# Sums of output-weight blocks by accumulating DRAM transfers; one sweep over both column halves

## The chip, the cores and the metric

The kernel runs on one core of a Trainium2 chip. The metric is the device time of one execution in microseconds; the median of several runs is given. An execution is also recorded by the profiler, and the views below are of such a recorded execution. The engines are called as the profile does: PE is TensorE (PEld its weight loads), DVE is VectorE, ACT is ScalarE, POOL is GpSimd, SP is SyncE, which here only issues transfers.

## The reference

One layer of a decoder trunk over 512 tokens of width 2048. The normalised input, modulated by a conditioning vector, goes through one input projection. Half of its columns feed a state-space (SSD) branch, half a retention branch. Both results side by side are 4096 wide, go through one output projection, are gated, added to the residual and normalised again.

```python
u = rms_norm(h, norm_w) * (1.0 + scale) + shift
proj = u @ w_in
z, xbc, dt_raw, q, k, v, g = jnp.split(proj, ...)
y_ssd = gated_group_rms_norm(ssd_chunked(...) + xs * d_skip, z, ssd_norm_w)
y_ret = head_group_norm(retention_chunked(...), ret_norm_w) * jax.nn.silu(g)
mixed = jnp.concatenate([y_ssd, y_ret], axis=-1) @ w_out     # (512, 4096) @ (4096, 2048)
h = h + gate[:, None, :] * mixed
return rms_norm(h, final_norm_w)
```

## The kernel before

All matrix products run in fp32 split in two: each operand is a high part (`hi`, the value cast to the matmul's fp32 form, on ACT) and a low part (`lo`, the rest, a subtraction on DVE). `mm3` multiplies hi by hi, hi by lo and lo by hi, three matmuls of 128 x 128 by 128 x 512 each.

The program text gives what is computed and in which buffers. A scheduler then orders each engine's instructions ahead of time on a simulated timeline: the earlier one in the text goes first, but one that is ready and has a buffer may go ahead of others that still wait. On the chip each engine runs its own list strictly in order, and waits where an operand is not there.

**Input projection** (`unit`, L109). A unit is 512 output columns. For each of 8 pairs of 128 rows of weight, `load_w` (L91) lets SP load 512 KB into one of three `raw` buffers, ACT writes one of four `hi`, DVE one of four `lo`; 24 matmuls follow. Nineteen units run through `unit`: first those of the SSD groups 1 to 3, each followed by `ssd_a` and `ssd_b`, then for each of four pairs of retention heads `qk`, `v` and `g` with `ret_a`, `ret_b` and `ret_c`. During the `v` units `gate_part` (L537) also loads the gate's weights through the `raw` buffers. POOL does short work for these branches: the decay loads `dec` from DRAM (L372), roots (L75, L76), the second half of the rotary sums (L439).

**Forms.** The output projection multiplies by a scheme with seven block products instead of eight (Strassen in Winograd's form). The operand of 4096 columns is taken in 16 blocks j of 256 columns, each with two halves of columns and two halves of tokens: A11, A12, A21, A22. `put_mix` (L327) builds the sums of these on POOL and stores them to DRAM (`mixd`): AS holds A11 and A21 - A22; SR, S2, A12 and A22 the others.

**Output projection** (L728 to L810). The 2048 output columns are taken as two halves q of 1024, and for each the whole scheme is run: per half 16 blocks, in each seven products of two row tiles. Three stretches follow each other for one q:

- a first loop with banks Y, Z and W: two neighbouring weight blocks are loaded into one `raw` of 512 KB, POOL adds them in place (L743) and makes the next sum `t2` from it (L748), then they are split (`split`, L698) and multiplied; `t2` stays in SBUF;
- a second loop: POOL adds a block to `t2` (L764) and builds another sum in `raw` (L770); the products add to Y, Z and W;
- a third loop multiplies A22 by `t2` into banks X.

The forms are loaded and split by `m_pair` (L711) in every stretch, once for each q: 112 splits of 128 x 512. `finish` (L659) multiplies by the gate, adds the residual and takes the sum of squares; `weighted` (L673) and `store` (L676) apply the last norm and send the row to DRAM. The finished tiles `h` have 16 buffers in the pool `res`, which opens when the branches' buffers are released.

Of the kernel before, what the change touches and what calls it, by code (L numbers as in the profile page):

```python
# [18 lines left out]
P = 128  # L19
# [22 lines left out]
def hybrid_block(ctx, tc, x, c_row, vecs, heads, w_mod, w_gate, b_gate, w_in, w_dt, w_out, fnw,  # L42
# [47 lines left out]

    def load_w(src, width, eng=dve):  # L91
        raw = wp.tile([P, 2, width], F32, tag="raw", bufs=3, name="raw")
        sp.dma_start(raw.rearrange("p k f -> p (k f)"), src)
        hi = wp.tile([P, 2, width], F32R, tag="hi", bufs=4, name="hi")
        lo = wp.tile([P, 2, width], F32R, tag="lo", bufs=4, name="lo")
        act.copy(hi, raw)  # L96
        eng.tensor_tensor(lo, raw, hi.bitcast(F32), ALU.subtract)  # L97
        return hi, lo
# [10 lines left out]
    def unit(name, w_stationary, tag="mm", side=None):  # L109
# [190 lines left out]
    def conv_silu(pb, ct, tag, bufs, name, r=None):  # L300
# [5 lines left out]
        for j in range(1, 4):  # L306
# [10 lines left out]
            for f, n in (("AS", 2 * QJ), ("SR", 2 * QJ), ("S2", QJ), ("A12", QJ), ("A22", QJ))}  # L317
# [9 lines left out]
    def put_mix(i, src, nw):  # L327
# [13 lines left out]
        s2 = t2k("xd", 2, "ms", (P, 256))  # L341
        pool.tensor_tensor(g[:, 0, :], a11, a21, ALU.subtract)
        pool.tensor_tensor(a21, a21, a22, ALU.subtract)
        pool.tensor_tensor(s2, a21, a11, ALU.subtract)
        pool.tensor_tensor(g[:, 1, :], a12, s2, ALU.add)
        pool.dma_start(mixd["AS"][j].rearrange("p a t -> p (a t)"), ma)
        pool.dma_start(mixd["SR"][j], g)
        pool.dma_start(mixd["S2"][j // 2][:, j % 2, :], s2)
        pool.dma_start(mixd["A12"][j // 2][:, j % 2, :], a12)
        pool.dma_start(mixd["A22"][j // 2][:, j % 2, :], a22)  # L350

# [300 lines left out]
    for n in range(4):  # L652
        fw = res.tile([P, 512], F32, tag=f"fw{n}", name=f"fw{n}")
        pool.dma_start(fw, fnw[n * 512:(n + 1) * 512].partition_broadcast(P))
        fws.append(fw)
# [3 lines left out]
    def finish(t, n, c, more=None):  # L659

        xr = t2k("zs", 4, "xr")
        sp.dma_start(xr, x[t * P:(t + 1) * P, n * 512:(n + 1) * 512])
        h = res.tile([P, 512], F32, tag="h", bufs=16, name=f"h{t}_{n}")
        if more is not None:
            dve.tensor_tensor(h, c, more, ALU.add)
            c = h
        dve.tensor_tensor(h, c, gate[n], ALU.mult)
        dve.tensor_tensor(h, h, xr, ALU.add)
# [4 lines left out]
    def weighted(t, n):  # L673
        dve.tensor_tensor(hout[t][n], hout[t][n], fws[n], ALU.mult)

    def store(t, late):  # L676
# [4 lines left out]
        for m in [late] + [m for m in range(4) if m != late]:  # L681
            h = hout[t][m]
            if m == late:
                dve.scalar_tensor_tensor(h, h, rs, fws[m], ALU.mult, ALU.mult)
            elif m == late ^ 1:
                dve.tensor_scalar(h, h, rs, None, ALU.mult)
            else:
                act.activation(h, h, AF.Copy, scale=rs)
# [9 lines left out]
    def split(dst, src, eng=dve):  # L698
        act.copy(dst[0], src)  # L699
        eng.tensor_tensor(dst[1], src, dst[0].bitcast(F32), ALU.subtract)  # L700

    def w_raw(q, jj, at):
        raw = wp.tile([P, 2, 512], F32, tag="raw", bufs=3, name="raw")
        sp.dma_start(raw.rearrange("p k f -> p (k f)"),
                     w_out[QJ * q + jj][:, at * 512:(at + 2) * 512])
        return raw

    def w_pair():
        return [wp.tile([P, 2, 512], F32R, tag=tg, bufs=4, name=tg) for tg in ("hi", "lo")]

    def m_pair(src):  # L711
        mr = t2k("xs", 5, "mr")
        sp.dma_start(mr, src.rearrange("p a t -> p (a t)"))
        mh = up.tile([P, 512], F32R, tag="ul", bufs=NK + 1, name="mh")
        ml = up.tile([P, 512], F32R, tag="ul", bufs=NK + 1, name="ml")
        split((mh, ml), mr)
        return mh, ml

    def mul(banks, m, i, w, k, first, last, rows=(0, 1), more=False):

        for t in rows:
            sl = slice(i * 256 + t * P, i * 256 + (t + 1) * P)
            mm3(banks[t], (m[0][:, sl], m[1][:, sl]), (w[0][:, k, :], w[1][:, k, :]), first, last, more)

    def kept_tile(tag):
        return res.tile([P, 512], F32, tag=tag, bufs=2, name=tag)

    for q in range(2):  # L728
        n0, n1 = 2 * q, 2 * q + 1
        by = [bank("mm", f"Y{t}") for t in range(2)]  # L730
        bz = [bank("mm", f"Z{t}") for t in range(2)]
        bw = [bank("aux", f"W{t}") for t in range(2)]
        t2s = []
        for jj in range(QJ):
            ms2 = m_pair(mixd["S2"][jj])
            t2w = w_pair()
            for e in range(2):
                first, last = jj == e == 0, jj == QJ - 1 and e == 1
                t2 = up.tile([P, 512], F32, tag="uh", bufs=NK, name="t2")
                sp.dma_start(t2, w_out[QJ * q + jj][:, (5 if e else 2) * 512:(6 if e else 3) * 512])  # L740
                raw = w_raw(q, jj, 6 * e)
                m = m_pair(mixd["AS"][2 * jj + e])
                pool.tensor_tensor(raw[:, 1 - e, :], raw[:, 0, :], raw[:, 1, :], ALU.add)  # L743
                w = w_pair()
                split(w, raw)
                mul(by, m, 0, w, e, first, last)
                mul(bw, m, 1, w, 1 - e, first, last)
                pool.tensor_tensor(t2, t2, raw[:, 1 - e, :], ALU.add)  # L748
                split([v[:, e, :] for v in t2w], t2)
                mul(bz, ms2, e, t2w, e, first, last)  # L750
                t2s.append(t2)
        e1, u2, w1 = ([kept_tile(tg) for _ in range(2)] for tg in ("e1", "u2", "w1"))
        for t in range(2):
            act.copy(e1[t], by[t])
            dve.tensor_tensor(u2[t], bz[t], e1[t], ALU.add)
            act.copy(w1[t], bw[t])
        for jj in range(QJ):
            raw = w_raw(q, jj, 3)
            m = m_pair(mixd["A12"][jj])
            w = w_pair()  # L760
            split(w, raw)
            for e in range(2):
                t2 = t2s[2 * jj + e]
                pool.tensor_tensor(t2, t2, raw[:, e, :], ALU.add)  # L764
                mul(by, m, e, w, e, False, jj == QJ - 1 and e == 1, more=True)
            for e in range(2):
                last = jj == QJ - 1 and e == 1
                raw = w_raw(q, jj, 5 if e else 1)
                m = m_pair(mixd["SR"][2 * jj + e])
                pool.tensor_tensor(raw[:, e, :], raw[:, 0, :], raw[:, 1, :], ALU.add)  # L770
                w = w_pair()
                split(w, raw)
                mul(bz, m, 0, w, e, False, last, more=True)
                mul(bw, m, 1, w, 1 - e, False, last, more=True)
        for t in range(2):
            finish(t, n0, by[t])
        for t in range(2):
            dve.tensor_tensor(e1[t], bz[t], e1[t], ALU.add)
            dve.tensor_tensor(u2[t], bw[t], u2[t], ALU.subtract)
            pool.tensor_tensor(w1[t], w1[t], e1[t], ALU.subtract)  # L780
            finish(t, n1, u2[t])
            finish(2 + t, n1, w1[t])
        if q:
            for t in range(2):
                weighted(t, n0)
                store(t, n1)
        bx = [bank("aux", f"X{t}") for t in range(2)]
        held = []
        for jj in range(QJ):
            m = m_pair(mixd["A22"][jj])  # L790
            w = w_pair()
            for e in range(2):
                split([v[:, e, :] for v in w], t2s[2 * jj + e])
            held.append((jj, m, w))
            if q and QJ - 3 <= jj < QJ - 1:
                continue
            for t in range(2):
                for jj_, m, w in held:
                    for e in range(2):
                        mul(bx, m, e, w, e, jj_ == e == 0, jj_ == QJ - 1 and e == 1, (t,))  # L800
            held = []
        for t in range(2):
            finish(2 + t, n0, bx[t], e1[t])
            if q:
                weighted(2 + t, n1)
                store(2 + t, n0)
        if not q:
            for t in range(NC):
                weighted(t, n0)
                weighted(t, n1)  # L810
# [27 lines left out]
def _quads(w):  # L838


    k, n = w.shape
    b = w.reshape(k // 512, 2, 2, P, n // 1024, 2, 512).transpose(4, 0, 3, 1, 2, 5, 6)
    order = [(0, 0, 0), (0, 0, 1), (0, 1, 1), (0, 1, 0), (1, 1, 0), (1, 1, 1), (1, 0, 1), (1, 0, 0)]
    return np.stack([b[:, :, :, e, i, j] for e, i, j in order], axis=3).reshape(-1, P, 8 * 512)
# [49 lines left out]
```

## Time and profile before

| | us |
|---|---|
| median of 3 runs | 1538.67 (1538.36 to 1545.83) |
| the profiled execution | 1534.36 |
| its span | 1532.6 |
| PE busy | 1448.2 |
| DVE busy | 1035.2 |
| ACT busy | 570.6 |
| POOL busy | 546.8 |
| bytes moved by all transfers | 263.30 MB |

A row of the groups reads: line, engine and operation, what is written and read with its shape, how often, then busy time in us and the mean ns of one, then the idle time of the engine just before these instructions and what ended it. A row of the waits reads: who waited, for what, us in total, how often, the longest. In the timeline the first two numbers are start and duration. A busy PE is not PE at its peak: a matmul of 512 columns is shown as 0.39 us long, but the next starts 0.23 us later.

### The profile page before, as it was taken

To read this page: it belongs to the slowest core of one execution; us is meant where nothing else is said; L and a number is where in the kernel's file an instruction comes from. 1 tells how busy PE (TensorE), PEld (TensorE's weight loads), DVE (VectorE), ACT (ScalarE), POOL (GpSimd) and SP (SyncE) were. 2 spreads that over 40 slices of the span, in tenths; PEclk is the share of its full clock that TensorE was granted. 3 is DMA by queue.
4 is the path that set the end of the run, shared out by engine and by line. 5 is a ranking of instruction groups with operands and counts; after the bars stand their busy time and mean duration, and the time that the engine had idled before them with its cause. 6 is when DMAs were issued, how large, how long until landed. Compare 5 with 4: busy or idle time off the path is not lost.

```text
span 1532.6 us, 17621 instructions
## 1 busy us (share of the span) xinstructions
PE 1448.2 (94%) x6481; PEld 1169.3 (76%) x6481; DVE 1035.2 (68%) x1160; ACT 570.6 (37%) x816; POOL 546.8 (36%) x512
## 2 busy tenths in 40 slices
PE   6988999999999999999999999999998898878895
PEld 4766887778888888888888888888886666656774
DVE  6899777775564574543544364336458998999897
ACT  6423443534433432223121322132235445544454
POOL 4540015562054144101300220022037767266662
PEclk9999999999999999999999999999999999999998
DMA  9888442534234225523552444245466677756763
GB/s 359 327 306 287 148 124 81 166 116 145 90 116 145 96 79 176 179 74 106 167 169 83 145 156 139 83 145 169 150 206 228 229 241 248 240 181 196 247 193 138
DMA packets 82810, 263.30 MB, mean 172 GB/s; under 512 B 10145, under 2 KB 10321, under 8 KB 78625
## 3 DMA queue, kind: packets, MB, share of 16 engines
q1 hardware_dynamic: 73298, 233.98, 46.7%
q0 software_dynamic: 8272, 26.08, 4.9%
q10 hardware_dynamic: 1152, 2.10, 0.4%
q8 instruction: 51, 0.84, 0.2%
q14 instruction: 37, 0.30, 0.1%
HBM read 243.18 MB, written 18.94 MB: 171 GB/s over the span
## 4 chain that ended last, share of the span: by engine, by line
PE 60%; DVE 12%; DMA 4%; POOL 4%; issue 3%; ACT 2%; POOLq 0%; DVEq 0%; ACTq 0%; SPq 0%
PE acc L105 16%; PE acc L107 16%; PE acc L106 16%; DVE lo L700 6%; DMA raw<-w_out_d 4%; DVE ml L700 2%; POOL raw L770 1%; PE py L390 1%; PE po L487 1%; ACT hi L699 1%; PE pT L332 1%; PE Y L106 1%; PE po L489 1%; PE pkv L508 1%; POOL t L764 1%
## 5 line engine op out<-in xcount | busy, mean ns | idle before, releaser
L97 DVE TENSOR_TENSOR lo<-raw,hi 128x1024 fp32r<-128x1024 f32 (+1 forms) x166 | 211.4, 1276 | 256.0 <-ACT hi L96 253.3
L96 ACT CAST hi<-raw 128x1024 fp32r<-128x1024 f32 (+1 forms) x184 | 186.4, 1017 | 440.9 <-PE acc L107 193.8
L106 PE MATMUL acc<-lo,uh 128*128 128x512 f32 x704 | 278.3, 395 | 0.0
L107 PE MATMUL acc<-hi,ul 128*128 128x512 f32 x704 | 276.5, 393 | 0.0
L105 PE MATMUL acc<-hi,uh 128*128 128x512 f32 x704 | 274.1, 392 | 0.4 <-ACT cr L303 0.4
L107 PE MATMUL acc<-uh,lo 128*128 128x512 f32 x512 | 200.2, 391 | 0.0
L106 PE MATMUL acc<-ul,hi 128*128 128x512 f32 x512 | 200.0, 391 | 0.0
L105 PE MATMUL acc<-uh,hi 128*128 128x512 f32 x512 | 199.9, 392 | 0.0
L700 DVE TENSOR_TENSOR lo<-raw,hi 128x1024 fp32r<-128x1024 f32 x80 | 146.1, 1827 | 14.5 <-ACT hi L699 14.3
L105 PEld LDWEIGHTS acc<-hi,uh 128*128 128x128 f32 x704 | 132.2, 188 | 27.6 <-ACT cr L303 0.6
L107 PEld LDWEIGHTS acc<-hi,ul 128*128 128x128 f32 x704 | 132.3, 188 | 27.6 <-issue 0.5
L106 PEld LDWEIGHTS acc<-lo,uh 128*128 128x128 f32 x704 | 132.2, 188 | 27.4 <-issue 0.5
L700 DVE TENSOR_TENSOR ml<-mr,mh 128x512 fp32r<-128x512 f32 x112 | 122.7, 1097 | 17.8 <-PE acc L107 11.2
L699 ACT CAST hi<-raw 128x1024 fp32r<-128x1024 f32 x80 | 84.0, 1050 | 104.3 <-POOL raw L770 68.4
L107 PEld LDWEIGHTS acc<-uh,lo 128*128 128x128 f32 x512 | 96.2, 188 | 19.6
L106 PEld LDWEIGHTS acc<-ul,hi 128*128 128x128 f32 x512 | 96.2, 188 | 19.5
L105 PEld LDWEIGHTS acc<-uh,hi 128*128 128x128 f32 x512 | 96.2, 188 | 19.4
L187 DVE SCALAR_TENSOR_TENSOR ada<-ada,csb 128x2048 f32<-128x2048 f32 x32 | 90.9, 2843 | 0.3 <-DMA ada<-w_mod_d 0.3
L550 DVE SCALAR_TENSOR_TENSOR gacc<-graw,cs,gacc 128x512 f32<-128x512 f32 x60 | 50.4, 841 | 57.2 <-DMA graw<-w_gate_d 56.1
L743 POOL TENSOR_TENSOR raw<-raw 128x512 f32<-128x512 f32 x32 | 54.7, 1710 | 82.1 <-DMA raw<-w_out_d 47.8
L75 POOL TENSOR_SCALAR mv<-mv 128x2 f32<-128x2 f32 x16 | 3.1, 191 | 204.6 <-DVE mv L496 204.6
L699 ACT CAST mh<-mr 128x512 fp32r<-128x512 f32 x112 | 68.4, 616 | 17.5 <-PE W L107 13.2
(264 smaller groups left out, 2655.4 us busy)
## 6 DMA issues: line engine op xcount, KB each, us to landing
raw<-w_out_d SPq DMA_DIRECT2D x80, 512.0 KB, 4.3
ada<-w_mod_d SPq DMA_DIRECT2D x32, 1024.0 KB, 5.8
raw<-w_in_z SPq DMA_DIRECT2D x32, 512.0 KB, 3.6
raw<-w_in_qk SPq DMA_DIRECT2D x32, 512.0 KB, 3.5
raw<-w_in_v SPq DMA_DIRECT2D x32, 512.0 KB, 3.9
graw<-w_gate_d SPq DMA_DIRECT2D x32, 512.0 KB, 3.7
raw<-w_in_g SPq DMA_DIRECT2D x32, 512.0 KB, 4.0
raw<-w_in_xs SPq DMA_DIRECT2D x24, 512.0 KB, 3.7
```

The costliest lines, as they stand in the source:

```text
L96: act.copy(hi, raw)
L97: eng.tensor_tensor(lo, raw, hi.bitcast(F32), ALU.subtract)
L105: pe.matmul(dst, lhsT=ah, rhs=bh, start=first, stop=False, skip_group_check=more)
L106: pe.matmul(dst, lhsT=ah, rhs=bl, start=False, stop=False, skip_group_check=more)
L107: pe.matmul(dst, lhsT=al, rhs=bh, start=False, stop=last, skip_group_check=more)
L187: dve.scalar_tensor_tensor(ada, ada, 0.5, csb, ALU.mult, ALU.mult, accum_out=dst)
L332: pe.transpose(pT[:, c * P:(c + 1) * P], src[c], ident)
L390: pe.matmul(py[:, hd], lhsT=dec[:, h, :], rhs=xd[:, hd], start=True, stop=True)
L550: dve.scalar_tensor_tensor(gacc, raw[:, kk, :], cs[:, k:k + 1], gacc, ALU.mult, ALU.add)
L699: act.copy(dst[0], src)
L700: eng.tensor_tensor(dst[1], src, dst[0].bitcast(F32), ALU.subtract)
L743: pool.tensor_tensor(raw[:, 1 - e, :], raw[:, 0, :], raw[:, 1, :], ALU.add)
```

## The change

The scheme and its number of matmuls stay. What changes is where the weight sums are made and how often things are split.

- **Weights in DRAM.** `_quads` lays out each block j as four tensors of 128 x 1024, B11, B12, B22 and B21, each with both column halves q side by side. `tsum` holds four sums for each j in DRAM: T1 = B11 + B12, T3 = B12 + B22, T2 = T1 + B22, T4 = T2 + B21.
- **Block sums by transfer.** `block_sums(n)` issues a staggered pipeline of six stages: SP copies B11 to T1 and B12 to T3; POOL adds B12 to T1 and B22 to T3 by an accumulating transfer; POOL copies T1 to T2; adds B22; copies T2 to T4; adds B21. `unit` calls it at every sixth weight load, and SP's copies are put behind that load in SP's list. A block enters at each call; 16 blocks are through after 21 calls.
- **Sweeps.** One pass over all 16 blocks serves both column halves and both row tiles, so there are four banks U and four banks W. The sweeps take (AS; B11, T1), (SR; T2, B22), (SA; T3, B21) for (U, W), and a last one A22 with T4 into U alone. U is not started anew: it keeps adding over all four sweeps, and what is needed of it between them is copied (`e1`, `u2`) or subtracted (`w1`).
- **Splits.** A weight is loaded and split once, 1024 wide, with no sum on POOL; a form is loaded and split once: 48 in the three sweeps and 8 in the last.
- **Buffers.** From the 25th weight on, the rings of `raw`, `hi` and `lo` have two more buffers each from `res`. `h` takes the buffers that `t2` had. `fnw` is loaded by SP during the first sweep instead of by POOL before it.
- **put_mix** writes SR and SA in place of SR, S2 and A12: the same number of additions and stores.

```diff
     def load_w(src, width, eng=dve):
...
-        sp.dma_start(raw.rearrange("p k f -> p (k f)"), src)
+        last_load[0] = sp.dma_start(raw.rearrange("p k f -> p (k f)"), src)
...
             if side is not None:
                 side(kc)
+            n = next(steps)
+            if n % 6 == 0:
+                with tc.issue_after(last_load[0].ins):
+                    block_sums(n // 6)
...
+    tsum = [[dram.tile([P, 1024], F32, name=f"T{i + 1}_{j}") for i in range(4)]
+            for j in range(2 * QJ)]
+    B11, B12, B22, B21 = (lambda j, i=i: w_out[4 * j + i] for i in range(4))
+    T1, T2, T3, T4 = (lambda j, i=i: tsum[j][i] for i in range(4))
...
+    def block_sums(n):
+        def add(dst, src):
+            pool.dma_start(dst, src, accum_op=ALU.add, max_dma_last_dim=4096)
+        stages = (
+            lambda j: (sp.dma_start(T1(j), B11(j)), sp.dma_start(T3(j), B12(j))),
+            lambda j: (add(T1(j), B12(j)), add(T3(j), B22(j))),
+            lambda j: pool.dma_start(T2(j), T1(j)),
+            lambda j: add(T2(j), B22(j)),
+            lambda j: pool.dma_start(T4(j), T2(j)),
+            lambda j: add(T4(j), B21(j)))
+        for i, stage in enumerate(stages):
+            if 0 <= n - i < 2 * QJ:
+                stage(n - i)
...
-    def finish(t, n, c, more=None):
+    def finish(t, n, c, more=None, op=ALU.add):
...
+        if n % 2:
+            dve.tensor_tensor(h, h, fws[n], ALU.mult)
...
+    ring = {"raw": (3, 2), "hi": (4, 2), "lo": (4, 2)}
+    def ring_tile(tag, dtype):
+        n, m = ring[tag]
+        used[tag] += 1
+        at = used[tag] % (n + m)
+        if used[tag] > 24 and at >= n:
+            return res.tile([P, 2, 512], dtype, tag=tag + "2", bufs=m, name=tag)
+        return wp.tile([P, 2, 512], dtype, tag=tag, bufs=n, name=tag)
...
+    def weight(src):
+        raw = ring_tile("raw", F32)
+        last_load[0] = sp.dma_start(raw.rearrange("p k f -> p (k f)"), src)
+        pair = [ring_tile(tg, F32R) for tg in ("hi", "lo")]
+        split(pair, raw)
+        return pair
...
+    for sweep, (f, wu, ww) in enumerate((("AS", B11, T1), ("SR", T2, B22), ("SA", T3, B21))):
+        if sweep != 1:
+            bw = {}
+        late = []
+        for j in range(NJ):
+            m = mixed(mixd[f][j])
+            mul(bu, m, 0, weight(wu(j)), sweep == j == 0, j == NJ - 1, sweep > 0)
...
+            late.append((j, m))
+            if sweep == 0 and j < 3:
+                continue
+            if not bw:
+                bw = {at: bank("aux", "W") for at in PAIRS}
+            for j_, m_ in late:
+                mul(bw, m_, 1, weight(ww(j_)), sweep != 1 and j_ == 0, j_ == NJ - 1, sweep == 1)
+            late = []
+        for at in PAIRS:
+            q, t = at
+            if sweep == 0:
...
+                act.copy(e1[at], bu[at])
+            elif sweep == 1:
+                u2 = res.tile([P, 512], F32, tag="u2", bufs=2, name="u2")
+                act.copy(u2, bu[at])
+                finish(t, 2 * q + 1, bw[at], u2, ALU.subtract)
+            else:
+                dve.tensor_tensor(w1[at], w1[at], bu[at], ALU.subtract)
...
+            elif sweep == 2:
+                finish(t, 2 * q, bw[at], e1[at])
+        if sweep == 2:
+            for at in PAIRS:
+                q, t = at
+                finish(2 + t, 2 * q + 1, w1[at])
+            for t in range(2):
+                store(t)
+    held = []
+    for j in range(NJ):
+        if j % 2 == 0:
+            m = mixed(mixd["A22"][j // 2])
+        held.append((j, m, weight(T4(j))))
+        if NJ - 3 <= j < NJ - 1:
+            continue
+        for at in PAIRS:
+            for j_, m_, w in held:
+                mul(bu, m_, j_ % 2, w, False, j_ == NJ - 1, True, [at])
         held = []
+    for t in range(2):
+        for q in range(2):
+            finish(2 + t, 2 * q, bu[q, t])
+        store(2 + t)
```

More of the change, by code (lines that the diff above doesn't have):

```diff
@@ L651, in hybrid_block @@
     fws = []
[L652 to L655, printed above, removed]
     sso = const.tile([P, NC, 4], F32, name="sso")
     hout = [[None] * 4 for _ in range(NC)]
-    def finish(t, n, c, more=None):
+    def finish(t, n, c, more=None, op=ALU.add):
         xr = t2k("zs", 4, "xr")
         sp.dma_start(xr, x[t * P:(t + 1) * P, n * 512:(n + 1) * 512])
-        h = res.tile([P, 512], F32, tag="h", bufs=16, name=f"h{t}_{n}")
+        h = up.tile([P, 512], F32, tag="uh", bufs=NK, name=f"h{t}_{n}")
         if more is not None:
-            dve.tensor_tensor(h, c, more, ALU.add)
+            dve.tensor_tensor(h, c, more, op)
             c = h
@@ L670, in finish, with store @@
         act.activation(jk, h, AF.Square, accum_out=sso[:, t, n:n + 1])
+        if n % 2:
+            dve.tensor_tensor(h, h, fws[n], ALU.mult)
         hout[t][n] = h
-    def weighted(t, n):
-        dve.tensor_tensor(hout[t][n], hout[t][n], fws[n], ALU.mult)
-    def store(t, late):
+    def store(t):
         rs = small.tile([P, 1], F32, name="rs")
@@ L680, in store @@
         rsqrt_into(rs, rs, 1.0 / D, EPS)
-        for m in [late] + [m for m in range(4) if m != late]:
+        for m in range(4):
             h = hout[t][m]
-            if m == late:
+            if m % 2 == 0:
                 dve.scalar_tensor_tensor(h, h, rs, fws[m], ALU.mult, ALU.mult)
-            elif m == late ^ 1:
-                dve.tensor_scalar(h, h, rs, None, ALU.mult)
             else:
@@ L711, in m_pair, with split @@
-    def m_pair(src):
+    PAIRS = [(q, t) for t in range(2) for q in range(2)]
+    ring = {"raw": (3, 2), "hi": (4, 2), "lo": (4, 2)}
+    used = dict.fromkeys(ring, 0)
+    def ring_tile(tag, dtype):
[5 more added lines that the diff above has]
+        return wp.tile([P, 2, 512], dtype, tag=tag, bufs=n, name=tag)
+    def split(dst, src):
+        act.copy(dst[0], src)
+        dve.tensor_tensor(dst[1], src, dst[0].bitcast(F32), ALU.subtract)
@@ L716, in m_pair @@
[L716 to L721, printed above, removed]
-            sl = slice(i * 256 + t * P, i * 256 + (t + 1) * P)
[L723 to L783, printed above, removed]
-            for t in range(2):
-                weighted(t, n0)
-                store(t, n1)
-        bx = [bank("aux", f"X{t}") for t in range(2)]
-        held = []
[L789 to L810, printed above, removed]
@@ new lines, in mixed, with mul @@
+        pair = [up.tile([P, 512], F32R, tag="ul", bufs=NK + 1, name=nm) for nm in ("mh", "ml")]
+        split(pair, mr)
+        return pair
+    def mul(banks, m, i, w, first, last, more=False, pairs=PAIRS):
+        for q, t in pairs:
+            sl = slice(i * 256 + t * P, i * 256 + (t + 1) * P)
+            mm3(banks[q, t], (m[0][:, sl], m[1][:, sl]), (w[0][:, q, :], w[1][:, q, :]),
+                first, last, more)
+    NJ = 2 * QJ
+    bu = {at: bank("mm", "U") for at in PAIRS}
+    bw = None
@@ L838, in _quads @@
 def _quads(w):
[L841 to L844, printed above, removed]
+    b = w.reshape(16, 2, P, 2, 2, 512).transpose(1, 4, 0, 2, 3, 5)
+    return np.stack([b[0, 0], b[0, 1], b[1, 1], b[1, 0]], axis=1).reshape(16 * 4, P, 1024)
 IN_UNITS = {"BC0": ((COL_B, 256), (COL_C, 256)), "xs0a": ((COL_XS, 256),), "z0": ((COL_Z, 512),),
@@ L875 @@
         "w_dt_d": a["w_in"][0][:, COL_DT:COL_Q].reshape(NK, P, HEADS).transpose(1, 0, 2),
-        "w_out_d": _quads(a["w_out"][0]),
         "fnw_d": a["final_norm_w"],
@@ L879 @@
     }
+    arrays["w_out_d"] = _quads(a["w_out"][0])
     for name, cols in IN_UNITS.items():
```

40 lines of the change are left out of this document (22 added, 18 removed).

## The prediction

> **What bounds the kernel now.** I read the stretches of the span first, then the waits of TensorE's weight loads, then the costliest groups, then what follows the last matmul. The columns of the first fence are: stretch, its length, then busy time and instructions of PE, PEld, DVE, ACT and POOL, the granted clock, the DMA share and GB/s.
>
> ```profile
> span 1532.6 us, 17621 instructions
> 600.00:700.00 100.00, 100.00 (x453) 83.03 (x453) 50.64 (x72) 20.85 (x23) 12.44 (x16) 1.00 0.40 127
> 1146.00:1303.00 157.00, 140.95 (x593) 108.51 (x592) 144.86 (x107) 79.32 (x114) 112.94 (x79) 0.99 0.73 237
> 1340.00:1486.00 146.00, 127.44 (x524) 99.03 (x523) 135.39 (x105) 69.35 (x99) 99.66 (x57) 0.96 0.69 215
> PEld Y L106 <- DVE lo L700: 28.9, 25, 3.0
> PEld Z L106 <- DVE lo L700: 12.7, 19, 1.4
> PEld X L106 <- DVE lo L700: 8.8, 8, 3.3
> PEld Y L105 <- ACT e L754: 6.3, 1, 6.3
> PEld Y L105 <- ACT hi L699: 4.9, 2, 4.6
> ```
>
> There are two regimes. In the input projection TensorE is busy for all of a 100 us stretch, with DVE half idle and the DMA share at 0.40: nothing can be won there, only lost. In the output projection (from 1146 us) DVE is busy 92 to 93% and TensorE is not; its weight loads wait for the `lo` half of a split. The five waits sum to 61.6 us (28.9 + 12.7 + 8.8 + 6.3 + 4.9), 50.4 of them on DVE.
>
> ```profile
> 1146.69 0.48 PE L105 MATMUL Y<-hi,mh 128*128 128x512 f32 x1
> 1157.73 0.39 PE L105 MATMUL W<-hi,mh 128*128 128x512 f32 x1
> 1161.58 0.39 PE L107 MATMUL W<-hi,ml 128*128 128x512 f32 x1
> 1516.41 0.39 PE L107 MATMUL X<-hi,ml 128*128 128x512 f32 x1
> ```
>
> Seventeen steps from 1157.73 to 1161.58 give 0.2265 us per matmul. The output projection has 2 x 16 x 14 x 3 = 1344 of them (seven block products of two row tiles, three matmuls each, 16 blocks, two column halves), so 304.4 us undisturbed. It runs from 1146.69 to 1516.8, 370.1 us. The difference, 65.7, is the waits of 61.6 and some transposes of the last heads. After the last matmul come 15.8 us of closing arithmetic and stores, which the change keeps in kind. So **the gain has a ceiling of about 62 us**.
>
> **What makes DVE late.**
>
> ```profile
> L97 DVE TENSOR_TENSOR lo<-raw,hi 128x1024 fp32r<-128x1024 f32 (+1 forms) x166 | 211.4, 1276 | 256.0 <-ACT hi L96 253.3
> L700 DVE TENSOR_TENSOR lo<-raw,hi 128x1024 fp32r<-128x1024 f32 x80 | 146.1, 1827 | 14.5 <-ACT hi L699 14.3
> L700 DVE TENSOR_TENSOR ml<-mr,mh 128x512 fp32r<-128x512 f32 x112 | 122.7, 1097 | 17.8 <-PE acc L107 11.2 <-issue 3.1 <-ACT m L334 1.9
> L700 DVE TENSOR_TENSOR lo<-t,hi 128x512 fp32r<-128x512 f32 x64 | 62.4, 1005 | 4.0 <-ACT hi L699 4.0
> L743 POOL TENSOR_TENSOR raw<-raw 128x512 f32<-128x512 f32 x32 | 54.7, 1710 | 82.1 <-DMA raw<-w_out_d 47.8 <-DMA xr<-x_d 15.6 <-DMA t<-w_out_d 12.0
> L748 POOL TENSOR_TENSOR t<-t,raw 128x512 f32<-128x512 f32 x32 | 53.5, 1675 | 2.0 <-DMA t<-w_out_d 0.3
> L764 POOL TENSOR_TENSOR t<-t,raw 128x512 f32<-128x512 f32 x32 | 56.4, 1782 | 30.5 <-DMA raw<-w_out_d 30.5
> L770 POOL TENSOR_TENSOR raw<-raw 128x512 f32<-128x512 f32 x32 | 56.1, 1760 | 17.0 <-DMA raw<-w_out_d 11.0 <-DVE lo L700 5.7
> 1488.93 1.21 DVE L700 TENSOR_TENSOR lo<-raw,hi 128x1024 fp32r<-128x1024 f32 x1
> 1490.07 0.68 DVE L700 TENSOR_TENSOR ml<-mr,mh 128x512 fp32r<-128x512 f32 x1
> ```
>
> The same subtraction takes 1276 ns in the input projection and 1827 among POOL's sums; late in the span, with POOL quiet, it is 1.21 us, and the half-wide one 0.68 instead of 1.10.
>
> **Part 1, removed.** POOL's 128 sums go (54.7 + 53.5 + 56.4 + 56.1 = 220.7 us), and with them the step "load, sum, split" becomes "load, split". Both column halves now use one split of each form: 56 form splits instead of 112. Weight splits stay equal in width: 7 x 16 = 112 of 1024, against 80 of 1024 plus 64 of 512. DVE's splits therefore go from 146.1 + 122.7 + 62.4 = 331.2 us to 112 x 1.21 + 56 x 0.68 = 174 us. The finishing operations are about 46 us, worked out below. DVE then has 220 us of work beside 304 of matmul, 72%. DVE stops being the bound and TensorE becomes it. I take 61.6 us as removed.
>
> **Part 2, added inside the output projection.** (a) Supply. Each block of a sweep needs two 512 KB weights and a 256 KB form per 24 matmuls (5.4 us), or 241 GB/s.
>
> ```profile
> raw<-w_out_d SPq DMA_DIRECT2D x80, 512.0 KB, 4.3
> q1 hardware_dynamic: 73298, 233.98, 46.7%
> L699 ACT CAST hi<-raw 128x1024 fp32r<-128x1024 f32 x80 | 84.0, 1050 | 104.3 <-POOL raw L770 68.4 <-POOL raw L743 12.7 <-DMA raw<-w_out_d 6.7
> ```
>
> A raw buffer is held 4.3 (landing) + 1.05 (cast) + 1.21 (subtraction) + about 0.7 of queueing, some 7.3 us. With three buffers that is one weight per 2.4 us, against 2.72 wanted; the first 24 weights have only these three, later ones five. It is just enough. Ends: 0 and 25 us (half of today's 50.4 on DVE); I take 6, near zero because DVE has 28% to spare.
>
> (b) The seams between sweeps. Their durations:
>
> ```profile
> L668 DVE TENSOR_TENSOR h<-h,xr 128x512 f32<-128x512 f32 x16 | 12.3, 778 | 0.0
> L674 DVE TENSOR_TENSOR h<-h,fw 128x512 f32<-128x512 f32 x12 | 8.8, 738 | 0.0
> L667 DVE TENSOR_TENSOR h<-h,gate 128x512 f32<-128x512 f32 x4 | 3.7, 955 | 0.0
> L665 DVE TENSOR_TENSOR h<-X,e 128x512 f32<-128x512 f32 x4 | 2.6, 680 | 0.0
> ```
>
> After the second sweep a finish is 0.68 + 0.955 + 0.78 + 0.74 = 3.15 us of DVE, and the fourth W bank is released after three of them and one subtraction, 10.1 us. TensorE has 12 U matmuls and three banks of W meanwhile (2.7 + 2.0). So 5.4 us are late if the order of the text is kept, 0 if the scheduler lets a further U block go first; I take 4. After the third sweep DVE has four subtractions (2.7), four finishes of 2.4, four of 2.2 and two rows to store (3.3), 24.4 us in all, ahead of the splits of the last sweep. The rings hold up to five split weights, 13.6 us of matmul, so 0 to 11 us are late. Today's two such crossings cost 8.8 us on X (row above); I take half, 4.4. After the first sweep the copies (0.6 each on ACT) fit under 12 matmuls: nothing. All finishes and stores together: 12.6 + 9.6 + 8.8 + 5.8 + 2.7 + 6.6 = 46 us.
>
> Output projection: 61.6 - 6 - 4 - 4.4 = **47 us gained**.
>
> **Part 3, added to the input projection.** Per block j: SP issues two copies, POOL six transfers (four adding, two copying), each 512 KB from DRAM to DRAM; times 16, that is 32 on SP and 96 on POOL. SP's cost nothing as far as the loads are early:
>
> ```profile
> SPq L93 <- DVE lo L97: 677.8, 133, 34.6
> 427.52 0.59 POOL L372 DMA_DIRECT2D dec<-acs_d  x1 [4.39 <-PE py L390]
> 443.29 1.90 PE L390 MATMUL py<-xd,dec 128*128 128x64 f32 x16
> dec<-acs_d POOLq DMA_DIRECT2D x16, 512.0 KB, 4.7
> POOL mv L75 <- DVE mv L496: 204.6, 16, 43.3
> ```
>
> SP waits 677.8 us for a free raw buffer. Three raw and four split pairs stand between a load and its use, so a load may be some 15 us late before TensorE sees it. That cover is thinner in the `v` units, where gate loads share the ring. Bytes: 128 transfers are 67 MB. At full share queue q1 moves 233.98 MB / (0.467 x 1532.6 us) = 327 GB/s, so copies alone would be 205 us of all engines, and 308 if an adding one counts twice. Over the 800 us in which they run that is 0.26 to 0.39 on top of about 0.38: 0.64 to 0.77, a level that the output projection runs at today (0.73).
>
> POOL pays 96 x 0.59 = 57 us of issue, in time that it waits today (204.6 us in one row alone). What stands behind these instructions on POOL are the root chains, the rotary sums and the decay loads. Now POOL also waits: each of a block's transfers needs the one before landed, so an instruction issued early holds POOL until then. A `dec` load shares the queue. It goes out at 427.52 and its matmuls run at 443.29. The chain behind it is 4.7 + 1.1 + 1.2 + 1.1 + 1.2 = 9.3 us, so about 6 us are spare: one transfer ahead is hidden, two are not. Sixteen such loads, perhaps a quarter meeting two transfers, at 2 to 5 us: some 6. For root and rotary chains behind a waiting POOL I add another 4. No row shows a DRAM to DRAM transfer or an adding one. The nearest are 4.3 and 4.7 us to land, so an adding one lies between one and two of these. Bounds of the whole part: 0 and 60 us (half of the 96 waits, each with 1.2 us of TensorE behind it); I take **10**, near the low end because a full raw ring hides most.
>
> The Trainium skill ("DMA: Bandwidth & Descriptors", Rules for kernel authors) says that an accumulating transfer reads its destination and writes it later. By it the upper byte count, 308 us, would be the right one and the sum above would not change by more than its range; no run here shows it yet.
>
> **Sum.** -47 + 10 = -37. The span goes from 1532.6 to about 1496 and the profiled execution from 1534.4 to 1497. The median of the runs shown, 1538.67, lies 4.3 above that execution, so I give 1501 for a median.
>
> **Rivals.** (1) *Adding transfers are slow.* Outside the loads' 0.38 there are 496 us of all engines in the 800; the 64 copies take 64 x 1.6 = 103 of them. Each of the 64 adding ones may then take 6.1 us, 3.8 times a copy. From there on every microsecond more costs 64, through POOL held in its waits and loads late behind them; at 7.5 us each, 90 - 47 = 43 us slower, about 1580. The same sign comes from 0.5 us of TensorE per POOL transfer (47 / 96). For it: no row shows such a transfer, and the scan chains run with little to spare. Against it: 0.6 of the DMA time is free. Chance 0.18.
>
> (2) *POOL cannot issue beside DVE.* If each issue were held for a DVE subtraction of 1.2 us, 96 x 1.2 = 115 us of POOL, perhaps a third in front of a scan: 38 us, and the gain falls to 9, about 1530. The `dec` issue of 0.59 beside a busy DVE speaks against it. The Trainium skill ("SBUF — State Buffer", the box on DVE blocking DMA) has such a rule, for descriptors of POOL's transfers while DVE holds the shared port; the row does not bear it out. Chance 0.05.
>
> (3) *The loads become the bound.* Weights and forms are 112 x 0.524 + 56 x 0.262 = 73.4 MB; at the 213 to 215 GB/s of today's second stretch they take 343 us, not 304. The gain is then 61.6 - 39 - 8 = 15, less 10: about 1534. For it: three raw buffers at first. Against: 237 GB/s at share 0.73. Chance 0.10.
>
> (4) *All hidden*: nothing lost in the input projection, few stalls, about 1480. Chance 0.12.
>
> **Chances.** Forecast (1485 to 1525) 0.55, the rivals as given. The measurement tells 0.5%, 7.7 us, from no change: faster (below 1531) is 0.55 + 0.12 and about half of (2) and (3), 0.74; within it 0.08; slower 0.18. The range runs from 1474 (the 62 us, all kept) to 1566, into rival 1.
>
> **What would show it.** After: POOL's sums gone, the `lo` subtraction near 1.21 us and `ml` near 0.68, DVE below 80% in the output projection, weight loads waiting under 20 us in all, first to last output matmul about 323 us. In the input projection TensorE still fully busy, `dec` landing under 10 us, the last input matmul at 1155 instead of 1146. A later start of the output projection by over 50 us, POOL waiting on its own transfers and a DMA share near 1 would prove me wrong, as would raw loads as the releaser of casts all through the sweeps.

## The result, and the profile after

The changed kernel is slower: 1548.54 us (median of 20 runs, 1541.25 to 1557.04) against 1536.62 (median of 20 runs of before), a ratio of 1.0075, 95% interval 1.0058 to 1.0092. The profiled span went from 1532.6 to 1545.9 us. 37 us faster was forecast.

First the page of the kernel after: span, busy time by engine, the chain that ended last (by engine, then by line), and the queues (q0 is POOL's).

```profile
span 1545.9 us, 17183 instructions
PE 1450.1 (94%) x6481; PEld 1177.1 (76%) x6481; DVE 890.8 (58%) x1064; ACT 539.5 (35%) x732; POOL 395.0 (26%) x472
PE 52%; DMA 22%; DVE 13%; issue 6%; POOL 5%; ACT 2%; SPq 0%; DVEq 0%; POOLq 0%; ACTq 0%
PE acc L108 9%; PE acc L107 9%; PE acc L109 9%; DMA T<-w_out_d 9%; DMA graw<-w_gate_d 5%; DVE ada L193 4%; DMA T<-T 4%; PE U L108 4%; PE U L109 4%; PE U L107 3%; PE W L107 3%; PE W L108 3%; PE W L109 3%; DVE lo L99 2%; DVE ul L210 1%
q1 hardware_dynamic: 66834, 245.52, 46.3%
q0 software_dynamic: 18192, 75.37, 20.1%
```

DVE and POOL have 144 and 152 us less to do, and the span is longer all the same. In the chain that ended last, DMA has 22%, where it had 4% in the kernel before; 13% are the transfers of the sums (`T<-w_out_d` and `T<-T`).

The stretches of the kernel after (length, busy time and instructions of PE, PEld, DVE, ACT, POOL, then granted clock, DMA share and GB/s), and the first groups of matmuls on U with their first and last start:

```profile
190.00:480.00 290.00, 259.64 (x1206) 209.21 (x1206) 174.50 (x201) 104.46 (x152) 125.94 (x148) 0.95 0.71 201
600.00:800.00 200.00, 185.67 (x829) 151.47 (x829) 87.90 (x113) 47.74 (x62) 60.81 (x86) 0.97 0.75 215
1224.00:1535.00 311.00, 307.97 (x1355) 253.94 (x1353) 200.68 (x219) 159.10 (x209) 18.31 (x24) 0.99 0.75 248
L107 PE MATMUL U<-hi,mh x256: 387/389/522, 1223.5 to 1534.0; 128*128 128x512 f32 x128
L109 PE MATMUL U<-hi,ml x256: 388/389/474, 1224.5 to 1534.4; 128*128 128x512 f32 x128
```

The first two stretches of the kernel before, for comparison:

```profile
190.00:480.00 290.00, 287.05 (x1397) 235.32 (x1397) 194.00 (x229) 121.19 (x176) 114.25 (x131) 1.00 0.36 118
600.00:800.00 200.00, 200.00 (x913) 166.11 (x913) 100.34 (x127) 45.91 (x52) 32.41 (x42) 1.00 0.45 144
```

The output projection now runs from 1223.5 to 1534.8, 311.3 us instead of 370.1. TensorE is busy for 308 us of it and DVE for 65%. So 58.8 us were won there. But it starts at 1223.5 instead of 1146.7: the input projection became 76.8 us longer. After the last matmul there are 11.1 us instead of 15.8. The sum is 76.8 - 58.8 - 4.7 = 13.3 us, which is the difference of the spans.

What TensorE waits for in the input projection of the kernel after (190 to 1225 us) is in the waits of its weight loads:

```profile
PEld py L419 <- DVE dec L407: 15.6, 1, 15.6
PEld pst L432 <- POOL xw L430: 15.0, 7, 5.2
PEld acc L107 <- DVE rt L467: 13.0, 7, 2.8
PEld pT L342 <- DVE y L457: 9.4, 7, 4.0
PEld pk L482 <- POOL r L468: 7.5, 7, 2.4
PEld pkv L537 <- DVE yr L529: 6.8, 1, 6.8
```

They are not waits for weights. They stand in the scan (`py`, `pst`), the rotary products (`rt`, `r`) and the norms (`y`, `yr`), all chains with a step on POOL. All such rows but those that end in "issue" sum to 73.5 us from 190 us to the start of the output projection. Before, they sum to 4.7, and the longest is this:

```profile
PEld pT L332 <- DVE y L428: 3.1, 2, 2.2
```

POOL's own waits in the kernel after, here from 190 to 1180 us, name its transfers (L366 adds, L371 and L373 copy):

```profile
POOL T L366 <- DMA T<-T: 107.3, 26, 7.0
POOL T L366 <- DMA T<-w_out_d: 95.9, 19, 19.3
POOL T L373 <- DMA T<-w_out_d: 69.8, 16, 6.3
POOL T L371 <- DMA T<-w_out_d: 49.8, 14, 9.5
```

That is 322.8 us. What it does is plainest early in the scan. ACT has a tile of decay values, `acsT`, ready at 219.3 us in the kernel after, and POOL is to send it to DRAM, from where the `dec` loads read it. First the kernel before, then four instructions of the kernel after:

```profile
220.50 0.55 POOL L617 DMA_DIRECT2D acs_d<-acsT  x1 [50.46 <-ACT acsT L615]
228.27 0.52 POOL L373 DMA_DIRECT2D T<-T  x1 [6.09 <-DMA T<-w_out_d]
235.27 0.80 POOL L366 DMA_DIRECT2D T<-w_out_d  x1 [6.47 <-DMA T<-T]
235.80 0.86 POOL L646 DMA_DIRECT2D acs_d<-acsT  x1
251.74 3.67 PE L419 MATMUL py<-xd,dec 128*128 128x64 f32 x16 [15.18 <-DVE dec L407]
```

The brackets give the idle time before each instruction and what ended it. In the kernel before, POOL has long waited for `acsT` and sends it at 220.50; in the kernel after it is held by its own transfers until 235.80. TensorE then stands still for 15.18 us, until `py` has its `dec`. The 16 matmuls of `py` take 3.67 us, against 1.90 before, and the granted clock from 250 to 270 us is 0.81: the stop costs more than its own length.

Not every such hold costs TensorE as much. POOL's timeline from 414 to 463 us:

```profile
414.07 0.53 POOL L371 DMA_DIRECT2D T<-T  x1 [3.90 <-DMA T<-w_out_d]
421.63 0.83 POOL L366 DMA_DIRECT2D T<-w_out_d  x1 [7.03 <-DMA T<-T]
428.76 0.52 POOL L373 DMA_DIRECT2D T<-T  x1 [6.30 <-DMA T<-w_out_d]
...
460.85 0.81 POOL L366 DMA_DIRECT2D T<-w_out_d  x1 [3.60 <-DMA T<-T]
461.41 1.32 POOL L430 TENSOR_TENSOR xw<-xd,dte 128x512 f32<-128x512 f32 x1
```

For 47 us POOL issues a transfer in half a microsecond to one, waits mostly 4 to 7 us for it to land, issues the next, which needs it, and so on through two blocks' chains. `xw` (a step of the scan) is behind them, and TensorE's `pst` at 462.78 waits for `xw`, but only 2.3 us: until then TensorE had matmuls of a unit to do. The six stages of a block were written six weight loads apart, but only SP's copies were tied to a load. POOL's were free, so the plan put each right behind the one that it needs.

### The profile page after: what moved, and what is told of

Its sections match the earlier page's. It is cut to its first block, busy times and chain, and to the rows that moved or that the text cites. A ratio compares the mean times of both kernels' runs of the same rounds, so it can differ in the third digit from the quotient of the medians.

```text
span 1545.9 us, 17183 instructions
## 1 busy us (share of the span) xinstructions
PE 1450.1 (94%) x6481; PEld 1177.1 (76%) x6481; DVE 890.8 (58%) x1064; ACT 539.5 (35%) x732; POOL 395.0 (26%) x472
## 3 DMA queue, kind: packets, MB, share of 16 engines
q0 software_dynamic: 18192, 75.37, 20.1%
HBM read 304.00 MB, written 86.05 MB: 252 GB/s over the span
## 4 chain that ended last, share of the span: by engine, by line
PE 52%; DMA 22%; DVE 13%; issue 6%; POOL 5%; ACT 2%; SPq 0%; DVEq 0%; POOLq 0%; ACTq 0%
PE acc L108 9%; PE acc L107 9%; PE acc L109 9%; DMA T<-w_out_d 9%; DMA graw<-w_gate_d 5%; DVE ada L193 4%; DMA T<-T 4%; PE U L108 4%; PE U L109 4%; PE U L107 3%; PE W L107 3%; PE W L108 3%; PE W L109 3%; DVE lo L99 2%; DVE ul L210 1%
## 5 line engine op out<-in xcount | busy, mean ns | idle before, releaser
L107 PE MATMUL acc<-hi,uh 128*128 128x512 f32 x704 | 277.5, 396 | 11.0 <-DVE rt L467 10.7
L735 DVE TENSOR_TENSOR lo<-raw,hi 128x1024 fp32r<-128x1024 f32 x112 | 137.6, 1234 | 81.2 <-ACT hi L734 81.2
L734 ACT CAST hi<-raw 128x1024 fp32r<-128x1024 f32 x112 | 117.6, 1054 | 126.7 <-PE W L109 53.8
L366 POOL DMA_DIRECT2D T<-w_out_d x64 | 55.3, 886 | 212.4 <-DMA T<-T 107.3
L108 PE MATMUL U<-lo,mh 128*128 128x512 f32 x256 | 99.8, 390 | 0.8 <-DVE lo L735 0.8
L109 PE MATMUL U<-hi,ml 128*128 128x512 f32 x256 | 99.6, 390 | 0.0
L107 PE MATMUL U<-hi,mh 128*128 128x512 f32 x256 | 95.2, 390 | 0.0
```

The source lines that it names most:

```text
L107: pe.matmul(dst, lhsT=ah, rhs=bh, start=first, stop=False, skip_group_check=more)
L108: pe.matmul(dst, lhsT=ah, rhs=bl, start=False, stop=False, skip_group_check=more)
L109: pe.matmul(dst, lhsT=al, rhs=bh, start=False, stop=last, skip_group_check=more)
L366: pool.dma_start(dst, src, accum_op=ALU.add, max_dma_last_dim=4096)
L735: dve.tensor_tensor(dst[1], src, dst[0].bitcast(F32), ALU.subtract)
```

## The experiments

Theory A: POOL, held in order by waits for its own transfers, delays the scan, rotary and norm chains. Theory B: the bytes of the transfers make other loads late. Theory C: the new plan of the output projection delays the end of the input projection. Times are medians; before was 1536 to 1537 us in every comparison. "Start" is the first matmul of the output projection.

**Every POOL transfer behind the load of its step** (`e1_stagger`). The edge is one of order in the plan only, not a wait on the chip:

```diff
+                for i in pinned:
+                    tc.add_manual_dep(i.ins, last_load[0].ins.name, NOSYNC, reason="stage")
+                pinned.clear()
...
-            pool.dma_start(dst, src, accum_op=ALU.add, max_dma_last_dim=4096)
+            pinned.append(pool.dma_start(dst, src, accum_op=ALU.add, max_dma_last_dim=4096))
```

(and the same for the two copies).

> The same transfers, but each POOL transfer is put in the plan behind the weight load of its own step, so that the one before it in its chain was issued six loads earlier. Theory A (POOL, which runs its list in order, is held by waits for its own transfers: 323 us of idle time before them, and the scan and rotary chains of TensorE behind it): idle time before the transfers under 80 us, weight loads of the input projection waiting under 30 us instead of about 77, first output matmul at 1160 to 1185 us instead of 1223, 1490 to 1510 us in all. Theory B (the bytes of the transfers make the decay, gate and weight loads late): nothing of that, first output matmul after 1205, 1535 to 1555 us.

Measured: 1516.02 us, ratio to before 0.9856 (0.9827 to 0.9886). Start at 1193.3. POOL's waits for its transfers fell to 57 us, most of them in the first of these rows; the wait in the second was 15.0 us in the kernel after:

```profile
POOL T L371 <- DMA T<-w_out_d: 44.9, 6, 21.5
PEld pst L437 <- POOL xw L435: 1.9, 2, 1.2
```

The same bytes, the same 96 issues and the same additions cost 30 us less, so A holds for these 30. But time and start are later than A expected, and the weight loads' waits (counted as above) are 35.1 us and not under 30, so something else is left.

**The sums alone, in the kernel before** (`e2_sums_only`): `block_sums` added, its results read by nothing.

> The kernel before with the block sums added to its input projection and used by nothing. Theories A and B both: first output matmul 65 to 85 us later than the 1146.7 of before, 1595 to 1620 us. Theory C (the delay comes from the new plan of the output projection, whose loads reach into the end of the input projection): under 20 us later, 1535 to 1560 us.

Measured in one run: 1626.3 us, start at 1238.4, 91.7 later than before, a little more than A and B expected. The harm is there, and larger than the 76.8 us, without any of the new output projection, so C falls as the main cause.

**The output projection alone** (`e3_outonly`):

```diff
-                with tc.issue_after(last_load[0].ins):
-                    block_sums(n // 6)
+                pass
...
-    T1, T2, T3, T4 = (lambda j, i=i: tsum[j][i] for i in range(4))
+    T1, T2, T3, T4 = B11, B22, B12, B21
```

> The kernel after without any block sum: the output projection reads plain blocks where it read sums, so its output is another product. Theories A and B: first output matmul back at 1140 to 1155 us, output projection unchanged at 311 us, 1465 to 1480 us. Theory C: first output matmul after 1190.

Measured: 1489.42 us, ratio 0.9681 (0.9657 to 0.9705). Start at 1163.0, 16 us later than in the kernel before although there is no transfer of sums at all; that lies between what A and B and what C expected. The stretches of this kernel show where:

```profile
190.00:480.00 290.00, 287.92 (x1395) 236.15 (x1395) 192.49 (x228) 120.32 (x176) 116.56 (x132) 0.99 0.36 118
600.00:800.00 200.00, 193.71 (x866) 160.25 (x865) 97.40 (x128) 43.59 (x49) 35.01 (x42) 0.98 0.42 138
PEld pk L481 <- POOL r L467: 7.1, 5, 2.2
PEld acc L107 <- DVE rt L466: 7.0, 5, 1.8
```

The state-space part is as dense as before; the retention part, 600 to 800 us, is not (before: 200.00 busy of 200, 913 matmuls). Its program text there is the same as before, the planned order isn't. So of the 76.8 us about 60 belong to the sums and 16 come without them. Of these 16, 14.1 are the two waits of the rotary chain shown last, which the kernel before had for 0.2 us. The kernel after has them for 7.5 and 13.0 us: two of its six long rows are there for the most part without any sum. Why the rotary chain is late in this plan was not tried.

**The traffic without POOL** (`e5_sp_copies`): eight independent copies of 512 KB per block, all on SP.

```diff
+        if n < 2 * QJ:
+            for i in range(8):
+                sp.dma_start(tsum[n][i], w_out[4 * n + i % 4])
```

> Eight plain copies of 512 KB per block on SP's queue into tiles that nothing reads, none on POOL, and no transfer that waits for another; the output projection reads plain blocks. As many bytes are written as by the sums, 33 MB fewer are read. Theory A: first output matmul at most 15 us later than without sums, 1465 to 1490 us. Theory B: at least 40 us later, over 1505 us.

Measured in one run: 1488.61 us, start at 1159.4. The stretches of this kernel:

```profile
190.00:480.00 290.00, 282.68 (x1349) 230.36 (x1349) 191.10 (x227) 118.14 (x174) 114.70 (x125) 0.98 0.65 218
600.00:800.00 200.00, 200.00 (x913) 166.25 (x912) 98.10 (x131) 44.02 (x51) 35.04 (x43) 1.00 0.74 251
```

At a DMA share of 0.74 and 251 GB/s TensorE stays fully busy from 600 to 800 us. Against B: 67 MB more in these 800 us cost nothing as a whole. It is not free in every stretch: from 190 to 480 us TensorE runs 46 matmuls fewer than without sums (some 10 us), and makes up 47 from 600 to 800 us, where this plan has less of the rotary waits.

**Six plain POOL copies per block, no chain, nothing added** (`e8_pool_copies`): two copies on SP, six on POOL into separate tiles, each behind its step's load; the output projection reads plain blocks.

> Six plain copies on POOL and two on SP per block, into tiles that nothing reads, each behind its step's load; nothing waits for another, nothing is added; the output projection reads plain blocks. Theory A: POOL has no idle time before these transfers; what is lost against no sums is the price of 96 POOL issues and of decay loads behind them: first output matmul at 1170 to 1195 us, 1495 to 1520 us. If the adding is what costs: as without sums, under 1170 and 1492 us.

Measured in one run: 1519.58 us, start at 1191.0, nearly the staggered kernel (1193.3), and 32 us later than with the same eight copies per block on SP (1159.4). POOL was not quite without such waits (14 us). So 96 transfers on POOL's queue cost this much without any adding. That the staggered kernel pays for nothing else is not shown: its loss stands elsewhere. Against the kernel without sums it ran 71 matmuls fewer from 190 to 480 us and 13 fewer from 600 to 800 us; here it is 43 and 79. A `dec` load landed within 6.5 us without sums, within 21.7 in the staggered kernel and 16.8 here, behind bursts on POOL's queue; but one took 14.3 us in `e5_sp_copies` too, with no such transfer there, so the queue alone is not shown to make it late.

**Four POOL transfers instead of six** (`e6_four`): SP also copies B22 to T2 and B21 to T4, POOL adds T1 to T2 and T2 to T4; the stages are seven loads apart, so that they spread over the steps.

```diff
+            lambda j: (sp.dma_start(T1(j), B11(j)), sp.dma_start(T3(j), B12(j)),
+                       sp.dma_start(T2(j), B22(j)), sp.dma_start(T4(j), B21(j))),
+            lambda j: (add(T1(j), B12(j)), add(T3(j), B22(j))),
+            lambda j: add(T2(j), T1(j)),
+            lambda j: add(T4(j), T2(j)))
...
+            j, r = divmod(n - 0 - 7 * i, 6)
```

> The sums with four transfers on POOL instead of six: SP copies B22 to T2 and B21 to T4 as well, POOL then adds T1 to T2 and T2 to T4; the stages stand at different loads, so that at most two POOL transfers are queued together, each in the plan behind its load. If what the staggered kernel still lost against no sums (first output matmul at 1193 instead of 1163 us) came from decay loads queued behind a burst of six transfers and from POOL's issue time: first output matmul at 1165 to 1180, decay loads landing under 8 us at worst, 1490 to 1505 us. If it came from the adding itself: as the staggered one, 1510 to 1520 us.

Measured: 1502.86 us, ratio 0.9772 (0.9753 to 0.9791). Start at 1178.1; `dec` landed within 10.6 us, a little above the 8 expected; 28 us of waits for own transfers.

**The same four, free in the plan** (`e9_four_unpinned`): the three lines with `add_manual_dep` taken out.

> The four POOL transfers per block, but free in the plan again, so that the scheduler may put each right behind the one it needs. Theory A (waits for own transfers hold POOL): three links per block instead of five, so about 130 to 220 us of idle time before POOL's transfers against 323 with six and 28 with four behind their loads; first output matmul at 1190 to 1210 us, 1515 to 1535 us. If the number of transfers and their burst alone made the difference: as with four behind their loads, 1500 to 1506 us.

Measured: 1514.35 us (0.9855, 0.9833 to 0.9878), start at 1193.1, and these waits of POOL:

```profile
POOL T L365 <- DMA T<-w_out_d: 206.3, 40, 20.3
POOL T L365 <- DMA T<-T: 78.0, 14, 8.1
```

284 us of waits, more than I expected, for a start 15 us later than with the edges, as expected (the time just under the 1515 expected): A again, though total waiting is a poor measure of the loss. What counts, as I read it, is how long one chain holds POOL and what is behind it; with three links a hold is shorter than with five.

**Four transfers, begun with the retention branch** (`e7_four_late`): `divmod(n - 56 - 6 * i, 5)`.

> The same four transfers, begun only with the first unit of the retention branch (a block every five loads), where no decay loads are on POOL's queue. If the decay loads of the state-space branch carry the rest of the loss: TensorE in 190 to 480 us as busy as without sums (288 us), first output matmul at 1163 to 1172 us, 1488 to 1498 us. If the rest is spread over all POOL work: first output matmul after 1180, since the gate loads and rotary sums now meet all transfers.

Measured: 1512.32 us (0.9841, 0.9809 to 0.9874), start at 1187.5. The first half of the expectation holds, TensorE in 190 to 480 us is busy for 287.92; the rest misses, and the start is after 1180, as the other half had it. The stretch from 800 us on and two loads show why:

```profile
800.00:1000.00 200.00, 184.57 (x805) 150.24 (x804) 82.47 (x119) 42.59 (x50) 42.64 (x56) 0.97 0.87 259
raw<-w_in_v SPq DMA_DIRECT2D x32, 512.0 KB, 8.0
graw<-w_gate_d SPq DMA_DIRECT2D x32, 512.0 KB, 6.9
```

Compressed into the retention part the transfers bring the DMA share to 0.87, and weights of the `v` units land in 8.0 us instead of 3.7 without sums. Unit matmuls then wait 17.9 us for weight splits (`hi` and `lo`); in the kernel after and without sums they have no such wait. Here theory B's mechanism is seen. It is seen, smaller, wherever POOL's transfers are tied to loads: these waits are 7.7 us in `e1_stagger`, 8.3 in `e8_pool_copies` and 9.7 in `e6_four`, and none in `e9_four_unpinned`.

**Four transfers, thinner** (`e10_four_thin`): a block every eight loads, every POOL transfer at a load of its own.

> Four POOL transfers behind their loads, a block every eight loads instead of six, SP's four copies at two places and every POOL transfer at a load of its own. If what is left (first output matmul at 1178 against 1163 us without sums) comes from transfers that meet in the queues: first output matmul at 1165 to 1173 us, 1490 to 1498 us. If it comes from POOL's issue time and from the order that the plan takes: as before, 1498 to 1506 us.

Measured: 1512.79 us (0.9847, 0.9826 to 0.9867), start at 1185.9, slower than at every six loads, although POOL waited only 8 us. Both expectations miss: it is worse than either. The sums reach further into the retention part, where DVE waited 127.7 us for gate loads (111.0 at every six). That this is the reason is not shown: unit matmuls waited 7.2 us for weight splits, less than the 9.7 at every six.

**Four transfers, none at the loads of the `v` units** (`e11_four_gap`):

```diff
+            if side is None:
+                n = next(steps)
+                with tc.issue_after(last_load[0].ins):
+                    block_sums(n)
```

> Four POOL transfers behind their loads, and no sums issued at the loads of the v units, where the gate loads share the raw buffers and DVE takes them in order (it waits 111 us for them with the sums beside them, 88 without). If these waits, which stand ahead of the rotary products on DVE, carry the rest of the loss: DVE's wait for gate loads under 95 us, first output matmul at 1165 to 1172 us, 1488 to 1497 us. If the rest is the order that each plan happens to take: 1498 to 1513 us, like the other versions with four.

Measured: 1492.33 us, ratio 0.9719 (0.9696 to 0.9742), start at 1168.0. The time is as expected, the sum of DVE's waits isn't: 109.6 us for gate loads, and not under 95. But that sum is the wrong measure, as POOL's was. What TensorE waited for did change. First two rows and an instruction of `e6_four`, then the row that is left here:

```profile
PEld acc L110 <- DVE lo L101: 7.0, 3, 3.3
PEld acc L109 <- ACT hi L100: 2.7, 2, 1.9
810.68 1.54 DVE L581 SCALAR_TENSOR_TENSOR gacc<-graw,cs,gacc 128x512 f32<-128x512 f32 x2 [7.56 <-DMA graw<-w_gate_d]
PEld acc L110 <- DVE lo L101: 1.9, 2, 1.5
```

In `e6_four` DVE, which runs its list in order too, stands before a gate load that is not there, and the split of the next weight stands behind it. The waits for weight splits fell from 9.7 to 1.9 us, 7.8 of the 10.1 us by which the start is earlier, and the gate loads' share of the chain that ended last from 7% to 4%, as without sums. So by these rows gate loads late at the `v` units account for most of the gain, though DVE's total hides it. This version beats both kernels, by 2.8% and 3.6% (1492.33 / 1548.54), and its start is 5 us behind the kernel without sums.

## Why the prediction was wrong

**The ceiling and the output projection: right, the gain too small.** The ceiling of 62 us was the right size: 58.8 were won, 47 forecast. (The lower end of the range, 1474, should have been 1477 by its own working, 1538.67 less 61.6.) The waits of weight loads behind a split are gone; in the whole output projection of the kernel after two are left:

```profile
PEld W L107 <- ACT m L344: 2.5, 1, 2.5
PEld U L108 <- DVE lo L735: 1.2, 1, 1.2
```

I had taken 6 us for supply and 8.4 for the seams. Both hid; as I read it, DVE's total of 201 us in these 311 leaves the splits ahead at the seams.

**DVE's durations: right.** The groups of the kernel after, in the output projection:

```profile
L735 DVE TENSOR_TENSOR lo<-raw,hi 128x1024 fp32r<-128x1024 f32 x112 | 137.6, 1234 | 81.2 <-ACT hi L734 81.2
L735 DVE TENSOR_TENSOR ml<-mr,mh 128x512 fp32r<-128x512 f32 x53 | 37.0, 700 | 29.7 <-PE W L108 20.4 <-PE acc L109 8.8 <-DMA mr<-mixSR 0.3
```

1234 and 700 ns against the 1.21 and 0.68 us taken, with POOL's sums gone.

**Rival 3, loads as the bound: fell.** 248 GB/s at a share of 0.75 fed 308 us of matmul.

**The tail** was forecast to stay; it became 4.7 us shorter.

**The step that failed is Part 3**, the input projection's loss taken as 10 us, "near the low end because a full raw ring hides most". It was 76.8 us, 60 of them the sums'. The ring hides late weight loads, and it did: in `e5_sp_copies` the `z` weights landed in 5.8 us instead of 3.5 and no unit matmul waited for a weight split. But the added wait was POOL's, and I had written down what stands behind it without pricing it as TensorE's list sees it. TensorE runs in order too. One `pst` or `py` that waits for POOL stops all unit matmuls behind it, as in the 15.18 us before 251.74. Four microseconds for the "root and rotary chains behind a waiting POOL" was the term; the sums cost about 60 (1223.5 against 1163.0). The upper bound of 60 was about what the sums cost here and too low for the whole part (76.8) and for the sums in the kernel before (91.7); I had chosen near its wrong end. I also read the six stages as the text spaces them, while the plan was free to close them up. Of the signs that I had named for being wrong, the late start and POOL waiting on its own transfers came; a DMA share near 1 did not.

The price of the rival was in the prediction: a loss from "0.5 us of TensorE per POOL transfer (47 / 96)". Measured are 60 / 96 = 0.63 us. I gave it as a second way to rival 1 and weighed it by the free DMA time, which doesn't bear on it.

**Rival 1's own mechanism, slow adding transfers: fell.** The issues of the kernel after, with their median time to landing:

```profile
T<-w_out_d POOLq DMA_DIRECT2D x64, 512.0 KB, 6.8
T<-w_out_d SPq DMA_DIRECT2D x32, 512.0 KB, 6.4
T<-T POOLq DMA_DIRECT2D x32, 512.0 KB, 5.0
```

An adding transfer lands in 6.8 us, a plain copy from DRAM to DRAM in 5.0 to 6.4. Queue q0's share rose from 4.9 to 20.1%, some 236 us of all engines (0.201 x 1545.9 - 0.049 x 1532.6) for 96 transfers, 2.5 us each on average; 6.1 was the point from which they would not fit. The DMA share of 0.71 to 0.76 was within what the byte counts gave (0.64 to 0.77).

**The decay loads: not late in the landing, but late in the issue.** They landed within 8.8 us in the kernel after, under the 10 that I named; one took 21.7 only once the chain was spread. What I had not priced is that the store of `acsT`, and the loads with it, go out late: 235.80 instead of 220.50.

**Rival 2, POOL unable to issue: not seen.** An adding issue takes POOL 0.86 us and a copy 0.52, with DVE busy for 60% of 190 to 480 us and 44% of 600 to 800. The box on DVE blocking DMA in the Trainium skill ("SBUF — State Buffer") speaks of DVE operations in a two-port mode; whether one ran beside these issues is not shown here, so the row neither confirms that rule nor speaks against it. (The rival's 1530 also leaves out the 10 us of Part 3, which rival 3's sum takes off.)

Of the 76.8 us, then: about 60 are the sums; of these, 30 are POOL held by its own transfers (1223.5 to 1193.3, `e1_stagger`), 25 more are 96 rather than 64 transfers on POOL's queue, how they are spread over it and their neighbourhood to the `v` units (1193.3 to 1168.0, together, `e11_four_gap`), 5 are left. Within the 25, 7.8 are waits for weight splits behind late gate loads (from `e6_four` to `e11_four_gap`). Of the 16 us without any sum, 14.1 are waits of the rotary chain; why that chain is late stays open. Each of these differences also compares two plans, and plans differ where the program text is the same: from 600 to 800 us 866 matmuls ran in `e3_outonly` and 913 in `e5_sp_copies`, some 10 us. So each figure may be off by about that, and the split of the 25 is not shown.

## What to carry to other kernels

Work moved to a queue of an engine that runs in order is not free because the engine is idle: ask what waits the moved instructions bring, what stands behind them on that engine, and which list of TensorE waits for it. If a chain of transfers is meant to be staggered, tie every link to a step, not only the first, look at which loads share that step, and issue the links that need no such engine from another queue. Measure such a part alone, added to the old kernel and taken out of the new one: against the kernel before, here that gave +90 us (1626.3) and -47 us (1489.4) where the whole showed only +12.

## What the hardware showed that I had not expected

- An adding transfer of 512 KB from DRAM to DRAM needs hardly longer to land than a copy (6.8 against 5.0 to 6.4 us), but 0.86 us of POOL to issue, against 0.52.
- The profile counts 304.00 MB read from HBM and 86.05 written, against 243.18 and 18.94 before. That is the 67.1 MB of sources more and 6.3 MB fewer of weights and forms: nothing is counted for the destinations that the 64 adding transfers (33.5 MB) read by the rule of the Trainium skill that the prediction cites ("DMA: Bandwidth & Descriptors"). The count neither confirms nor excludes it.
- 67 MB of plain copies on SP's queue cost nothing as a whole, at a DMA share of 0.74 from 600 to 800 us (`e5_sp_copies`). With the sums squeezed into the retention part and a share of 0.87, unit matmuls waited 17.9 us for weight splits (`e7_four_late`).
- After a stop TensorE can be slower for a while: in `e6_four`, after 2.65 us of idle time, ten matmuls from 820.08 to 823.92 us start 0.43 us apart and those from 824.28 on 0.23. The granted clock was 0.51 from 819 to 824.3 us and 1.00 from 824.3 to 830.
